# One version of an expert's last block, branch hints on TensorE, and row sums on TensorE in a decoder step

## The chip, the cores and the metric

The kernel runs on one core of a Trainium2 chip. The metric is the time of one execution on the device in microseconds (us). A core has TensorE (PE, with its weight loads PEld), VectorE (DVE), ScalarE (ACT), GpSimd (POOL), and SyncE (SP), which here only starts transfers. Each engine has its own stream of instructions, and they meet by semaphores.

## The reference

One step of a one-layer decoder for a prompt of 2048 rows and 8 x 4 sample rows, all of width 1024. The attention and the state-space part come first; the change touches what follows them, a mixture of experts and the final norm:

```python
grp = argmax(softmax(hf @ w_rc + b_rc));  top_v, top_i = top_k(fine logits of grp, 2)
eid = grp * 8 + top_i                     # two of 32 experts for each row
hid = silu(xb @ w_gate[e]) * (xb @ w_up[e]);  ys = hid @ w_down[e]      # widths 1024 -> 512 -> 1024
y = sum of a row's two expert rows, times their gates
x = x + gate * y                          # gate: a vector from the conditioning
out = rms_norm(x, g_final)
```

## The kernel before

The expert stage (function `moe`) goes through the 32 experts in an order that the counts decide at run time. An expert's rows are cut into blocks of 128; `blocks[p]` is the number of rows of the p-th expert, read into a register of every engine. A block is 48 products into PU (`up`, 24 for each half `hf` of the hidden width), 24 into PO (`down`), 8 turns of the next block's rows (`turned`) and 4 of the hidden values (`hidT`). Every f32 product is three products in a faster format, so each weight unit is split into a high and a low part: ACT casts (L1940), DVE subtracts (L1941); `convert` does both, and after every second unit SP loads the next expert's part into the same buffer (`load`). An expert has 12 units. EARLY (0 to 3) and LATE (10, 11, of the expert before) can be converted only when the expert before is nearly through.

An expert with more than 128 rows first runs one to three blocks by `further` (branches L2109, L2111, L2113), then its last block by `main(p, True)`. An expert with at most 128 rows runs `main(p, False)` in the Else branch, a second copy of the same 84 PE instructions. The two copies differ in this: with several blocks the first `further` block has already converted the six units LATE and EARLY. Tile's framework counts semaphores the same on every path: where an `If` is skipped, each engine raises the counts that the skipped instructions would have raised. Instructions stand in the order of the code on each engine (a manual schedule).

Stored rows go to Y_d by POOL's indirect transfers. The last stage (function `final`) takes 17 tiles of 128 rows (the last has 32): DVE adds the two rows of each row's experts (L2258) and multiplies by the gate (L2259), POOL adds x (L2260; DVE in the last three tiles), ACT sums the squares (L2265), DVE and POOL make 1/rms (L56, L58), DVE scales (L2270), and ACT's queue stores. It is a pipeline of three tiles: `add(n)`, `square(n - 1)`, `store(n - 2)`.

Of the kernel before, what the change touches and what calls it, by code (L numbers as in the profile page):

```python
# [12 lines left out]
F32 = mybir.dt.float32  # L13
# [4 lines left out]
ALU = mybir.AluOpType  # L18
AX = mybir.AxisListType
PSUM = bass.MemoryType.PSUM  # L20
# [1861 lines left out]
STEPS = (), (0, 1, 2, 3, 4, 5), (6,), (7,), (), (), (8, 9)  # L1882
EARLY = 0, 1, 2, 3
BOTH, AT0, AT1 = 4, 6, 1
LATE = 10, 11


class Experts:
# [20 lines left out]
    def load(self, p, i):  # L1909

        if p >= 32:
            self.after(i)
            return
        if not self.ready:
            self.later.append((p, i))
            return
        if i in (0, 5):
            self.now = self.K.nc.sync.value_load(self.R.order[0:1, p:p + 1], min_val=0, max_val=31)
        load_w(self.K, self.I, self.RAW[i], bass.ds(self.now, 1), i)

# [9 lines left out]
    def convert(self, p, u, hi, lo):  # L1930

        h = u % 2
        raw = self.RAW[u // 2]
        wh, wl = self.unit(p, u)
        if u < 8:
            raw = raw.rearrange("p (j k f) -> p j k f", j=2, k=2)[:, :, h]
            wh, wl = (t.rearrange("p (j f) -> p j f", j=2) for t in (wh, wl))
        else:
            raw = raw[:, 1024 * h:1024 * h + 1024]
        hi(wh, raw)  # L1940
        lo.tensor_tensor(out=wl, in0=raw, in1=wh.bitcast(F32), op=ALU.subtract)  # L1941
        if h:
            self.load(p + 1, u // 2)


def moe(K, I, E, first, h2_d, Y_d, R, TK, last):
# [4 lines left out]
    tc, nc = K.tc, K.nc  # L1951
    V, G, A = nc.vector, nc.gpsimd, nc.scalar
    NE = 32
    with ExitStack() as st:
# [15 lines left out]
        def convert(p, us):  # L1970
            for u in us:
                if p < NE:
                    E.convert(p, u, A.copy, V)
# [54 lines left out]
            nc.gpsimd.indirect_dma_start(out=Y_d, out_offset=bass.IndirectOffsetOnAxis(ap=R.dst[:, col:col + 1], axis=0),  # L2028
                                         in_=Y, in_offset=None, bounds_check=2 * TK - 1, oob_is_err=False)

        def block(p, before, x, steps):


            for k in range(BOTH):
                up(p, 0, (k,))
                up(p, 1, (k,))
            steps[0]()
            if before is not None:
                store(before)
            steps[1]()  # L2040
            up(p, 0, range(BOTH, 8))
            act(0)
            if x is not None:
                turned(x)
            steps[2]()
            up(p, 1, range(BOTH, AT0))
            hidT(0)
            up(p, 1, range(AT0, 8))
            steps[3]()
            act(1)  # L2050
            steps[4]()
            if x is not None:
                prepare()
            steps[5]()
            for c in range(AT1):
                down(p, c)
            hidT(1)
            steps[6]()
            for c in range(AT1, 4):
                down(p, c)  # L2060
# [4 lines left out]
        def further(p, b):  # L2065


            steps = [nothing] * 7
            if b == 0:
                steps[0] = lambda: convert(p, LATE)  # L2070
                steps[1] = lambda: convert(p + 1, EARLY)
            else:
                steps[1] = lambda: gather(R.src[:, 32 * (b + 1) + p:32 * (b + 1) + p + 1], X1)
            before = 32 * (b - 1) + p if b else 96 + p - 1
            block(p, before if p or b else None, X1, steps)

        def count(p):
            if p < NE:
                blocks[p] = nc.values_load(R.cnt[0:1, p:p + 1], min_val=0, max_val=2080)

        def main(p, several):

            def step(i):
                def run():
                    if i == 0 and not several:
                        convert(p, LATE)
                    elif i == 1:
                        gather_second(p + 1)
                    elif i == 2:
                        gather_first(p + 2)  # L2090
                    convert(p + 1, [u for u in STEPS[i] if not (several and u in EARLY)])
                return run

            block(p, 64 + p if p or several else None, X0 if p + 1 < NE else None, [step(i) for i in range(7)])

        gather(R.src0, X0)
        E.begin()
# [5 lines left out]
        blocks = {}  # L2103
        count(0)
        for p in range(NE):
            if p == NE - 1:
                last()
            count(p + 1)
            with tc.If(blocks[p] > 128) as several:  # L2109
                further(p, 0)  # L2110
                with tc.If(blocks[p] > 256):  # L2111
                    further(p, 1)
                    with tc.If(blocks[p] > 384):  # L2113
                        further(p, 2)
                main(p, True)
            with several.Else():
                main(p, False)
        store(96 + NE - 1)


# [116 lines left out]
def final(K, F, Y_d, TK, O):  # L2237
    tc, nc = K.tc, K.nc
    V, G, A = nc.vector, nc.gpsimd, nc.scalar
    with ExitStack() as st:  # L2240
        q = st.enter_context(tc.tile_pool(name="oq", bufs=10, reuse_waits="tile"))
        sm = st.enter_context(tc.tile_pool(name="os", bufs=4, reuse_waits="tile"))
        jk = q.tile([128, 1024], BF, name="jk", bufs=1)
        gfin, gate = F.place(0), [F.place(1), F.place(2)]
        tiles = {}

        def loads(n):
            t = F.seq[n]
            r = NS if t == 16 else 128
            y = [q.tile([128, 1024], F32, name=f"y{k}") for k in range(2)]  # L2250
            for k in range(2):
                nc.sync.dma_start(out=y[k][:r], in_=Y_d[TK * k + 128 * t:TK * k + 128 * t + r])  # L2252
            x = F.place(3 + n) if n < 9 else F.more[n - 9]
            tiles[n] = t, r, x, y

        def add(n):
            t, r, x, y = tiles[n]
            V.tensor_tensor(out=y[0][:r], in0=y[0][:r], in1=y[1][:r], op=ALU.add)  # L2258
            V.tensor_tensor(out=y[0][:r], in0=y[0][:r], in1=gate[t == 16][:r], op=ALU.mult)  # L2259
            (V if n > 13 else G).tensor_tensor(out=x[:r], in0=x[:r], in1=y[0][:r], op=ALU.add)  # L2260

        def square(n):
            t, r, x, y = tiles[n]
            ss = sm.tile([128, 1], F32, name="ss")
            A.activation(jk[:r], x[:r], AF.Square, accum_out=ss[:r])  # L2265
            rs[n] = rstd_of(K, sm, ss[:r], D)

        def store(n):
            t, r, x, y = tiles.pop(n)
            V.scalar_tensor_tensor(out=x[:r], in0=x[:r], scalar=rs.pop(n)[:r], in1=gfin[:r], op0=ALU.mult, op1=ALU.mult)  # L2270
            dst = O['ys'] if t == 16 else O['yp'].rearrange("(n t) d -> t n d", t=16)[t]
            nc.scalar.dma_start(out=dst, in_=x[:r])  # L2272

        N, rs = len(F.seq), {}
        for n in range(10):
            loads(n)
        for n in range(N + 2):
            for f, m in ((add, n), (square, n - 1), (store, n - 2)):
                if 0 <= m < N:
                    f(m)  # L2280
            if n + 10 < N:
                loads(n + 10)
# [114 lines left out]
```

## Time and profile before

| | |
|---|---|
| median of 3 runs | 2761.41 us (2761.29 to 2764.57) |
| profiled execution, its own time | 2763.94 us |
| its span | 2762.1 us |
| busy: PE, DVE, ACT, POOL | 2389.0, 1472.9, 1153.3, 568.4 us |
| expert stage, first product to last | 1622.83 to 2649.2 us |
| last stage | from there to 2762.1 us |

The span is the time from the first to the last instruction that the profiler saw; the execution's own time lies 1.8 us above it. Matmuls overlap: a product of 512 columns has a record of 0.39 us, and the next starts 0.23 us after it. [...] "issue" as a releaser says that nothing in the profile explains the wait.

### The profile page before, as it was taken

Reading aid. Unit: us, or ns where it says so; the run is one execution under the profiler, and the core shown is the slowest. Engines: PE = TensorE matmul, PEld = TensorE weight load, DVE = VectorE, ACT = ScalarE, POOL = GpSimd, SP = SyncE. Lnnn points to the kernel's source line nnn. Section 1 sums busy time; section 2 is a strip of 40 time slices with the busy share of each in tenths; the row PEclk is TensorE's granted clock in tenths of the full one; section 3 lists DMA queues with packets and bytes.
Section 4 is the critical chain, followed back from the end, with each engine's and each line's share of the span. In section 5 each row is a group of like instructions: output and inputs, shape, how many; then the busy total and the mean of one; then the engine's idle time right before and its main releaser. Section 6 shows DMA issues by size and latency. Waiting matters only on the chain. (4 is left out here: it accounts for less than half of the span.)

```text
span 2762.1 us, 35592 instructions
## 1 busy us (share of the span) xinstructions
PE 2389.0 (86%) x11999; PEld 1886.4 (68%) x11999; DVE 1472.9 (53%) x2980; ACT 1153.3 (42%) x1885; POOL 568.4 (21%) x725
## 2 busy tenths in 40 slices
PE   6999999897699999997999768999999998898930
PEld 3766677663367799995777647777777777777720
DVE  4544311264153566635687673544754676656558
ACT  3222211232133455555344353444654566556411
POOL 0022100001002335452444211101110111101036
PEclk9999999898899999998999879999999999999975
DMA  7322211575744621114333463645855786677664
GB/s 271 91 104 105 93 58 54 184 240 180 204 138 141 197 63 35 30 39 150 122 125 125 163 234 112 237 152 206 292 196 186 277 299 250 243 267 259 247 225 179
DMA packets 239150, 467.92 MB, mean 169 GB/s; under 512 B 87620, under 2 KB 117492, under 8 KB 236799
## 3 DMA queue, kind: packets, MB, share of 16 engines
q1 hardware_dynamic: 211496, 411.95, 43.4%
q0 software_dynamic: 16160, 38.50, 4.0%
q10 hardware_dynamic: 11200, 13.83, 1.5%
q8 instruction: 150, 2.46, 0.4%
q14 instruction: 144, 1.18, 0.1%
HBM read 395.60 MB, written 87.92 MB: 175 GB/s over the span
## 5 line engine op out<-in xcount | busy, mean ns | idle before, releaser
L1941 DVE TENSOR_TENSOR wl<-raw,wh 128x1024 fp32r<-128x1024 f32 x384 | 451.8, 1222 | 151.4 <-ACT wh L1940 145.9
L1940 ACT CAST wh<-raw 128x1024 fp32r<-128x1024 f32 x384 | 381.2, 1050 | 43.5 <-PE pu L2006 39.5
L2006 PE MATMUL pu<-wh,xh 128*128 128x512 f32 x816 | 340.8, 418 | 66.7 <-issue 52.6
L2006 PE MATMUL pu<-wl,xh 128*128 128x512 f32 x816 | 329.9, 404 | 5.0 <-issue 5.0
L2006 PE MATMUL pu<-wh,xl 128*128 128x512 f32 x816 | 329.3, 404 | 0.0
L2006 PEld LDWEIGHTS pu<-wh,xh 128*128 128x128 f32 x816 | 158.7, 195 | 110.9 <-issue 77.9
L206 PE MATMUL po<-wh,hh 128*128 128x512 f32 x512 | 208.6, 408 | 12.1 <-ACT hh L133 12.1
L206 PE MATMUL po<-wl,hh 128*128 128x512 f32 x512 | 206.9, 404 | 0.0
L206 PE MATMUL po<-wh,hl 128*128 128x512 f32 x512 | 202.7, 401 | 0.0
L2028 POOL DMA_INDIRECT Y_d<-y,Rdst x51 | 58.7, 1152 | 632.4 <-ACT y L2027 616.5
L2006 PEld LDWEIGHTS pu<-wl,xh 128*128 128x128 f32 x816 | 159.0, 195 | 37.1 <-issue 5.4
L2006 PEld LDWEIGHTS pu<-wh,xl 128*128 128x128 f32 x816 | 158.5, 194 | 37.1
L873 DVE CUSTOM_DVE_ANT_0 jk<-pa,mask 128x256 bf16<-128x256 f32 (+1 forms) x384 | 118.0, 362 | 113.7 <-PE pa L870 112.7
L2010 DVE TENSOR_TENSOR hid<-hid,pu 128x256 f32<-128x256 f32 x102 | 42.7, 419 | 241.8 <-ACT hid L2009 241.8
L2023 PE MATMUL po<-wh,hh 128*128 128x512 f32 x408 | 164.9, 404 | 0.0
L2023 PE MATMUL po<-wh,hl 128*128 128x512 f32 x408 | 160.3, 393 | 0.0
L2023 PE MATMUL po<-wl,hh 128*128 128x512 f32 x408 | 160.3, 393 | 0.0
L939 PE MATMUL pb<-QS,KH 128*128 128x256 f32 (+1 forms) x384 | 150.4, 398 | 0.0
L216 ACT COPY ob<-po 128x512 f32<-128x512 f32 x64 | 37.6, 587 | 264.1 <-PE po L206 262.2
L2009 ACT ACTIVATE hid<-pu 128x256 f32<-128x256 f32 x102 | 39.3, 385 | 254.1 <-PE pu L2006 253.4
L942 ACT ACTIVATE PT<-pb 128x512 f32<-128x512 f32 (+1 forms) x152 | 89.9, 591 | 120.3 <-PE pb L940 119.1
L940 PE MATMUL pb<-QM,KL 65*128 65x256 f32 (+1 forms) x384 | 139.2, 370 | 0.9 <-DMA QM<-MR 0.9
(586 smaller groups left out, 5035.1 us busy)
## 6 DMA issues: line engine op xcount, KB each, us to landing
raw<-w_expert_gate SPq DMA_DIRECT2D x128, 512.0 KB
raw<-w_expert_up SPq DMA_DIRECT2D x128, 512.0 KB
raw<-w_expert_down SPq DMA_DIRECT2D x64, 1024.0 KB
y<-Y_d SPq DMA_DIRECT2D x32, 512.0 KB
kr<-cache_k_win SPq DMA_DIRECT2D x56, 256.0 KB
kr<-cache_v_win SPq DMA_DIRECT2D x56, 256.0 KB
vb<-out_vp SPq DMA_DIRECT2D x96, 128.0 KB
wada<-w_ada_ffn SPq DMA_DIRECT2D x24, 512.0 KB
```

Of the source, the lines that this page charges most:

```text
L206: nc.tensor.matmul(out, a[:, kt, :], wt[c][:, kt], start=(kt == 0 and i == 0), stop=(kt == 7 and i == len(terms) - 1))
L873: V.tensor_tensor_reduce(out=jk[:, o:o + n], in0=pt[:, o:o + n], in1=mask[:, 256 - n:256], op0=ALU.add, op1=ALU.max, scale=1.0, scalar=-3e ...
L939: nc.tensor.matmul(po, cols(KH, c0, step, 128), cols(QS, c0, step, nq), start=True, stop=False)
L940: nc.tensor.matmul(po, cols(KL, c0, step, 128), cols(QM, c0, step, nq), start=False, stop=True)
L942: A.activation(PT[:, :o], ps[:, :o], AF.Exp)
L1940: hi(wh, raw)
L1941: lo.tensor_tensor(out=wl, in0=raw, in1=wh.bitcast(F32), op=ALU.subtract)
L2006: nc.tensor.matmul(PU[hf], x[:, k, :], y, start=(k == 0 and j == 0), stop=(k == 7 and j == 2))
L2009: A.activation(HID[hf], PU[hf][:, 0:256], AF.Silu)
L2010: V.tensor_tensor(out=HID[hf], in0=HID[hf], in1=PU[hf][:, 256:512], op=ALU.mult)
L2023: nc.tensor.matmul(PO[i], x[:, c % 2, :], y[:, cs], start=(c == 0 and j == 0), stop=(c == 3 and j == 2))
L2028: nc.gpsimd.indirect_dma_start(out=Y_d, out_offset=bass.IndirectOffsetOnAxis(ap=R.dst[:, col:col + 1], axis=0), in_=Y, in_offset=None, bou ...
```

## The change

The Else copy is gone. `main(p)` follows the `If` for every expert, and the six units LATE and EARLY are converted in it under a condition of their own (`alone`), in its first step; it always stores the block before. TensorE gets a hint instruction in each block behind which a branch on a count follows, with the count's comparison in a register. In the last stage PE adds the two expert rows by products with the unit matrix into PSUM (`both`), DVE multiplies from PSUM, and DVE adds x in all tiles; POOL has only the power left.

```diff
@@ -1914,7 +1914,7 @@
         if not self.ready:
             self.later.append((p, i))
             return
-        if i in (0, 5):
+        if i in (0, 2, 5):
             self.now = self.K.nc.sync.value_load(self.R.order[0:1, p:p + 1], min_val=0, max_val=31)
         load_w(self.K, self.I, self.RAW[i], bass.ds(self.now, 1), i)
 
@@ -2028,7 +2028,7 @@
             nc.gpsimd.indirect_dma_start(out=Y_d, out_offset=bass.IndirectOffsetOnAxis(ap=R.dst[:, col:col + 1], axis=0),
                                          in_=Y, in_offset=None, bounds_check=2 * TK - 1, oob_is_err=False)
 
-        def block(p, before, x, steps):
+        def block(p, before, x, steps, label, hint):
 
 
             for k in range(BOTH):
@@ -2052,6 +2052,8 @@
             if x is not None:
                 prepare()
             steps[5]()
+            if label:
+                tc.mark_branch_hint_location(label, hint=hint, engines=[mybir.EngineType.PE])
             for c in range(AT1):
                 down(p, c)
             hidT(1)
@@ -2072,26 +2074,33 @@
             else:
                 steps[1] = lambda: gather(R.src[:, 32 * (b + 1) + p:32 * (b + 1) + p + 1], X1)
             before = 32 * (b - 1) + p if b else 96 + p - 1
-            block(p, before if p or b else None, X1, steps)
+            at = 128 * (b + 2)
+            block(p, before if p or b else None, X1, steps, f"at{at}_{p}" if b < 2 else None, blocks[p] > at)
 
         def count(p):
             if p < NE:
                 blocks[p] = nc.values_load(R.cnt[0:1, p:p + 1], min_val=0, max_val=2080)
 
-        def main(p, several):
+        def main(p):
+
+            def alone():
+                with tc.If(blocks[p] <= 128):
+                    convert(p, LATE)
+                    convert(p + 1, EARLY)
 
             def step(i):
                 def run():
-                    if i == 0 and not several:
-                        convert(p, LATE)
+                    if i == 0:
+                        alone()
                     elif i == 1:
                         gather_second(p + 1)
                     elif i == 2:
                         gather_first(p + 2)
-                    convert(p + 1, [u for u in STEPS[i] if not (several and u in EARLY)])
+                    convert(p + 1, [u for u in STEPS[i] if u not in EARLY])
                 return run
 
-            block(p, 64 + p if p or several else None, X0 if p + 1 < NE else None, [step(i) for i in range(7)])
+            block(p, 64 + p, X0 if p + 1 < NE else None, [step(i) for i in range(7)],
+                  f"at128_{p + 1}" if p + 1 < NE else None, blocks[p + 1] > 128 if p + 1 < NE else None)
 
         gather(R.src0, X0)
         E.begin()
@@ -2106,15 +2115,13 @@
             if p == NE - 1:
                 last()
             count(p + 1)
-            with tc.If(blocks[p] > 128) as several:
+            with tc.If(blocks[p] > 128, label=f"at128_{p}"):
                 further(p, 0)
-                with tc.If(blocks[p] > 256):
+                with tc.If(blocks[p] > 256, label=f"at256_{p}"):
                     further(p, 1)
-                    with tc.If(blocks[p] > 384):
+                    with tc.If(blocks[p] > 384, label=f"at384_{p}"):
                         further(p, 2)
-                main(p, True)
-            with several.Else():
-                main(p, False)
+            main(p)
         store(96 + NE - 1)
 
 
@@ -2240,6 +2247,7 @@
     with ExitStack() as st:
         q = st.enter_context(tc.tile_pool(name="oq", bufs=10, reuse_waits="tile"))
         sm = st.enter_context(tc.tile_pool(name="os", bufs=4, reuse_waits="tile"))
+        ps = st.enter_context(tc.tile_pool(name="ops", bufs=4, space=PSUM, reuse_waits="tile"))
         jk = q.tile([128, 1024], BF, name="jk", bufs=1)
         gfin, gate = F.place(0), [F.place(1), F.place(2)]
         tiles = {}
@@ -2253,11 +2261,19 @@
             x = F.place(3 + n) if n < 9 else F.more[n - 9]
             tiles[n] = t, r, x, y
 
+        def both(n):
+
+            t, r, x, y = tiles[n]
+            zs[n] = ps.tile([128, 1024], F32, name="z")
+            for h in range(2):
+                cs = slice(512 * h, 512 * h + 512)
+                for k in range(2):
+                    nc.tensor.matmul(zs[n][:r, cs], K.ident[:r, :r], y[k][:r, cs], start=(k == 0), stop=(k == 1))
+
         def add(n):
             t, r, x, y = tiles[n]
-            V.tensor_tensor(out=y[0][:r], in0=y[0][:r], in1=y[1][:r], op=ALU.add)
-            V.tensor_tensor(out=y[0][:r], in0=y[0][:r], in1=gate[t == 16][:r], op=ALU.mult)
-            (V if n > 13 else G).tensor_tensor(out=x[:r], in0=x[:r], in1=y[0][:r], op=ALU.add)
+            V.tensor_tensor(out=y[0][:r], in0=zs.pop(n)[:r], in1=gate[t == 16][:r], op=ALU.mult)
+            V.tensor_tensor(out=x[:r], in0=x[:r], in1=y[0][:r], op=ALU.add)
 
         def square(n):
             t, r, x, y = tiles[n]
@@ -2271,11 +2287,12 @@
             dst = O['ys'] if t == 16 else O['yp'].rearrange("(n t) d -> t n d", t=16)[t]
             nc.scalar.dma_start(out=dst, in_=x[:r])
 
-        N, rs = len(F.seq), {}
+        N, rs, zs = len(F.seq), {}, {}
         for n in range(10):
             loads(n)
+        both(0)
         for n in range(N + 2):
-            for f, m in ((add, n), (square, n - 1), (store, n - 2)):
+            for f, m in ((both, n + 1), (add, n), (square, n - 1), (store, n - 2)):
                 if 0 <= m < N:
                     f(m)
             if n + 10 < N:
```

Three places in the order of instructions, without times. The first is PE where a single expert's block begins (the Else copy before; wh0 is the high part of a weight unit, xh the rows). Before:

```order
L2023 MATMUL po1_13300<-wh11_13283,hh1_13309 128x512
L2023 MATMUL po1_13300<-wl11_13284,hh1_13309 128x512
L2023 MATMUL po1_13300<-wh11_13283,hl1_13310 128x512
L2109 UNCONDITIONAL_BRANCH
L2006 MATMUL pu0_13297<-wh0_12952,xh_13301 128x512
L2006 MATMUL pu0_13297<-wl0_12953,xh_13301 128x512
```

and now, at the end of the skipped `If` and the start of `main`:

```order
L2023 MATMUL po1_13300<-wl11_13284,hh1_13309 128x512
L2023 MATMUL po1_13300<-wh11_13283,hl1_13310 128x512
L2122 UNCONDITIONAL_BRANCH
L2122 UNCONDITIONAL_BRANCH [waits PE_49]
L2120 UNCONDITIONAL_BRANCH [waits PE_49]
L2118 UNCONDITIONAL_BRANCH [waits PE_49]
L2006 MATMUL pu0_13297<-wh0_12952,xh_13301 128x512 [waits DVE_49,Activation_49]
L2006 MATMUL pu0_13297<-wl0_12953,xh_13301 128x512
```

The Else copy began with its first product and no wait; now the path that skips L2118 ends in a row that waits for PE's own semaphore, so for its products before, and `main` follows.

The second is PE in the middle of a single expert's block, where the products into PO begin. Before:

```order
L2006 MATMUL pu1_13298<-wh7_12947,xh_13301 128x512
L2006 MATMUL pu1_13298<-wl7_12948,xh_13301 128x512
L2006 MATMUL pu1_13298<-wh7_12947,xl_13302 128x512
L2023 MATMUL po0_13299<-wh8_13277,hh0_13307 128x512 [waits Activation_49]
L2023 MATMUL po0_13299<-wl8_13278,hh0_13307 128x512
```

and now:

```order
L2006 MATMUL pu1_13298<-wh7_12947,xh_13301 128x512
L2006 MATMUL pu1_13298<-wl7_12948,xh_13301 128x512
L2006 MATMUL pu1_13298<-wh7_12947,xl_13302 128x512
L2056 REGISTER_ALU
L2403 BRANCH_PREFETCH_HINT
L2023 MATMUL po0_13299<-wh8_13277,hh0_13307 128x512 [waits Activation_49]
L2023 MATMUL po0_13299<-wl8_13278,hh0_13307 128x512
```

A comparison of the next count and the hint stand ahead of the last 24 products of the block.

The third is ACT at a single expert's first casts (raw5 holds LATE, raw0 and raw1 hold EARLY; DMAHW are the semaphores of SP's transfers). Before:

```order
L1940 CAST wh0_12952<-raw4_12791 128x1024 [waits DMAHW6_49]
L1940 CAST wh1_12954<-raw4_12791 128x1024
L2109 UNCONDITIONAL_BRANCH
L1940 CAST wh6_12945<-raw5_12793 128x1024 [waits DMAHW5_49]
L1940 CAST wh7_12947<-raw5_12793 128x1024
L2027 ACTIVATE y_13305<-po0_13299,Rg_76 128x512 [waits DMASW3_49,DMASW2_49,DMASW5_49,PE_49,Activation_49]
L2027 ACTIVATE y_13305<-po1_13300,Rg_76 128x512 [waits PE_49,Activation_49]
L1940 CAST wh8_13277<-raw0_12779 128x1024 [waits DMAHW7_49,DMAHW6_49]
```

and now:

```order
L2118 UNCONDITIONAL_BRANCH [waits Activation_49]
L2087 COMPARE_AND_BRANCH
L1940 CAST wh6_12945<-raw5_12793 128x1024 [waits DMAHW1_49,DVE_49,DMAHW6_49,PE_49,Activation_49]
L1940 CAST wh7_12947<-raw5_12793 128x1024 [waits DVE_49,PE_49,Activation_49]
L1940 CAST wh8_13277<-raw0_12779 128x1024 [waits DMAHW2_49,DMAHW3_49,DMAHW0_49,DMAHW7_49,DVE_49,Activation_49]
L1940 CAST wh9_13279<-raw0_12779 128x1024 [waits DVE_49,Activation_49]
L1940 CAST wh10_13281<-raw1_12782 128x1024 [waits DMAHW2_49,DMAHW4_49,DMAHW1_49,DMAHW5_49,DVE_49,Activation_49]
L1940 CAST wh11_13283<-raw1_12782 128x1024 [waits DVE_49,Activation_49]
```

The casts of LATE waited for one transfer. They now wait also for DMAHW6, DVE and PE, whose counts SP, DVE and PE raise for the skipped `If`; the two ACTIVATEs that empty PO stand behind the six casts and no longer between them. SP's row for the skipped `If` (L2118) waits for SP_sequencer and five of its transfer semaphores.

## Rows read from the trace of the kernel before

**Rows 1.** Two stages: length, busy of PE PEld DVE ACT POOL, PEclk, DMA, GB/s.

```profile
1616.00:2649.60 1033.60, 953.25 (x4280) 763.08 (x4278) 586.51 (x696) 549.16 (x784) 115.17 (x100) 0.97 0.65 233
2649.60:2762.00 112.40, 0.00 (x0) 0.00 (x0) 94.68 (x71) 20.29 (x36) 70.91 (x32) 0.51 0.62 228
```

**Rows 2.** Waits of PE, 1600 to 2660: who, releaser, us in total, times, longest us.

```profile
PE pu L2006 <- issue: 57.7, 20, 5.0
...
PE pu L2006 <- PEq L2111: 5.9, 7, 1.9
...
PE pu L2006 <- PEq L2113: 1.1, 2, 0.5
```

**Rows 3.** Branch lines L2109 and L2111: count, ns min/median/max, first and last start.

```profile
L2109 PEldq COMPARE_BRANCH  x44: 70/310/6798, 1615.9 to 2646.5; - x44
...
L2109 POOLq INC_SWDGE_SEM  x20: 581/1022/1457, 1635.0 to 2566.4; - x20
...
L2111 PEldq COMPARE_BRANCH  x12: 65/1833/4585, 1658.8 to 2627.4; - x12
```

**Rows 4.** Timeline of PE at block starts: start, us, operation, [idle before, releaser].

```profile
1719.97 0.51 PE L2006 MATMUL pu<-wh,xh 128*128 128x512 f32 x1 [3.41 <-issue]
...
1725.51 0.80 PE L2006 MATMUL pu<-wl,xh 128*128 128x512 f32 x1 [5.03 <-issue]
...
1865.09 0.50 PE L2006 MATMUL pu<-wh,xh 128*128 128x512 f32 x1 [1.70 <-issue]
...
2553.94 0.80 PE L2006 MATMUL pu<-wh,xh 128*128 128x512 f32 x1 [3.76 <-issue]
...
2593.85 0.47 PE L2006 MATMUL pu<-wh,xh 128*128 128x512 f32 x1 [0.30 <-PEq L2111]
```

**Rows 5.** Short stretches behind a branch, within a block, and of one block.

```profile
1843.00:1846.70 3.70, 3.68 (x9) 2.91 (x10) 3.27 (x3) 2.45 (x3) 0.00 (x0) 0.55 1.02 395
1847.00:1850.40 3.40, 3.40 (x16) 2.81 (x15) 2.23 (x2) 1.05 (x1) 0.00 (x0) 1.00 0.98 375
...
1865.10:1883.50 18.40, 18.15 (x84) 14.75 (x85) 14.76 (x18) 13.07 (x18) 4.06 (x3) 1.00 1.00 375
```

**Rows 6.** Timeline of ACT, SP, DVE and PE around the block from 1865.09.

```profile
1861.45 1.99 ACT L1940 CAST wh<-raw 128x1024 fp32r<-128x1024 f32 x2
...
1863.02 2.68 SPq L1877 DMA_DIRECT2D raw<-w_expert_down  x2
...
1865.57 6.90 DVE L1941 TENSOR_TENSOR wl<-raw,wh 128x1024 fp32r<-128x1024 f32 x6 [0.31 <-ACT wh L1940]
...
1875.64 0.38 PE L2014 MATMUL pt<-ident,hid 128*128 128x128 f32 x2
```

**Rows 7.** Line L2109 on SP, from 1862 to 1868.

```profile
L2109 SPq COMPARE_BRANCH  x1: 55/55/55, 1864.0 to 1864.0; - x1
```

**Rows 8.** Timeline of the last stage: its first add, one of 13 slow tiles, the end.

```profile
2658.16 1.22 DVE L2258 TENSOR_TENSOR y<-y,y 128x1024 f32<-128x1024 f32 x1 [11.21 <-DMA y<-Y_d]
...
2682.03 3.38 POOL L2260 TENSOR_TENSOR raw<-raw,y 128x1024 f32<-128x1024 f32 x1 [0.93 <-DVE ms L56]
2683.13 3.36 DVE L2258 TENSOR_TENSOR y<-y,y 128x1024 f32<-128x1024 f32 x1
...
2742.32 1.22 DVE L2258 TENSOR_TENSOR y<-y,y 128x1024 f32<-128x1024 f32 x1
...
2747.23 1.21 DVE L2258 TENSOR_TENSOR y<-y,y 32x1024 f32<-32x1024 f32 x1
...
2749.72 1.21 DVE L2260 TENSOR_TENSOR x<-x,y 32x1024 f32<-32x1024 f32 x1
```

**Rows 9.** Timeline of PE: two f32 products of an earlier stage.

```profile
697.83 0.38 PE L700 MATMUL pt<-sa,UT 128*128 128x128 f32 x2
698.05 0.60 PE L701 MATMUL pt<-sb,HP 128*128 128x256 f32 x2
```

**Rows 10.** Group of instructions: DVE operation that reads PSUM; busy us, mean ns, idle before.

```profile
L134 DVE TENSOR_TENSOR xl<-pt,xh 128x512 fp32r<-128x512 f32 x102 | 65.5, 683 | 1.1
```

## The prediction

> **What bounds the kernel now.** I read the busy times of the two stages first, then PE's waits in the expert stage, then the branches behind them, then the blocks one by one, and last the final stage.
>
> The expert stage lasts 1033.6 us with PE busy for 953, while DVE and ACT are busy for little over half of it [rows 1]: PE bounds it, and what PE waits for is the loss. PE's waits there are mostly "issue": 57.7 us in 20 waits, then 5.9 and 1.1 us that its own sequencer ends at L2111 and L2113 [rows 2]. They are the branches on the counts. A branch that falls through takes PE's sequencer 70 ns, one that jumps to the far Else copy 4 to 6 us [rows 3]. The sequencer runs some 2 us ahead of the array, so part is hidden. Of 32 experts 12 reach L2111 and so have several blocks; POOL evens its counts 20 times, once for each single expert [rows 3]. A single expert behind an expert with several blocks finds PE idle for 3.4 to 3.8 us (ten such starts; the first and the last are shown), one behind another single expert for about 1.7 [rows 4]. One wait of 5.03 us is not at a branch but one product behind a jump [rows 4].
>
> A long wait costs twice. Behind it the granted clock is 0.55 and PE starts 9 products in 3.7 us, where it starts 16 in 3.4 at 1.0 [rows 5]: 9 would take 1.9, so 1.8 us are lost. After the short waits this doesn't happen (1.00 in the block from 1865.1) [rows 5].
>
> The last stage, 112 us, is bound by DVE, busy for 94.7; PE does nothing there and its clock is at the lower level [rows 1]. While POOL adds x (3.38 us), DVE's first addition beside it takes 3.36, where it takes 1.22 when POOL doesn't add [rows 8].
>
> **The branches on PE: what goes.** Idle time: 57.7 + 5.9 + 1.1 - 5.0 (the wait that isn't at a branch) = 59.7 us. Lower clock: 10 x 1.8 = 18. Together 77.7 us, if every branch found its target in time. The hint stands ahead of 24 products of 0.23 us, so 5.6 us, and some turns, before the block's end; the jumps took 4.1 to 5.9 us, at most 6.8 [rows 3]. That is just enough. The trace of before has no hint, so its effect is bounded by nothing and by all of it. The middle copy's branch (L2087) is a short one inside a block and hidden by the sequencer's lead; without that cover it would cost 0.3 us each, 10 us in all.
>
> **What comes in its place.** First, the path that skips the `If` now waits for PE's own products. The nearest rows are the skips at L2111 and L2113: 0.30 us idle where the branch was quick [rows 4], 0.55 and 0.84 on the mean of [rows 2]. I take 0.5: 20 single experts and 10 skips at 256 and 384 rows give 15 us.
>
> Second, and this the diff doesn't show: the casts of LATE in a single expert wait for a count that SP raises when it skips. SP comes there late, since it stands in order behind the load of raw4. Around the block from 1865.09 PE ended the block before at about 1863.4 (1865.09 less 1.70) [rows 4]; call this T. SP issued raw4 at 1863.02 and passed the branch at 1864.0 [rows 6, 7], T + 0.6. Jump and counting I put at 0.5 (no row shows it; POOL's counting takes 1.0 [rows 3], nothing is the other end). So the casts begin at T + 1.1; before they began at 1861.45 [rows 6], T - 1.95. DVE's eight subtractions (LATE, EARLY, units 4 and 5) stand ahead of its first product of the hidden values. At 1.15 us each [rows 6], one cast of 1.0 behind the first, they end at T + 11.3, and with 0.4 for that product hidT can start at T + 11.7. PE would reach hidT 10.55 us after the block's start [rows 6], so at T + 11.0. It waits 0.7, with POOL's price for the counting 1.2; I take 1.0 for 20 blocks: 20 us. The bounds are nothing and 1.6 us each. Behind DVE in that block nobody else waits: EARLY is used a block later, and PO, which ACT now empties after the six casts, is needed only 12 us into the block.
>
> The expert stage: 77.7 - 15 - 20 = 43 us less. The duties of the several-block path (the same casts, the same loads) are as before.
>
> If the hints did nothing, every single expert would pay the short wait of 1.7 (the jump over the Else copy, which makes ten of them long, is gone in any case): 10 x 2.0 + 18 = 38 us go, 4 come, and SP's lateness hides in the wait. That is 34 us less: the two outcomes lie close.
>
> **The last stage.** PE adds the rows by four products of 512 columns with f32 operands. An earlier f32 product of 128 columns took 0.22 us from start to start, in two records, at the full clock [rows 9]; four of 512 columns take 16 times that, 3.5 us for a tile, and 7.0 at the lower clock. DVE keeps three operations: the multiplication, now from PSUM, the addition of x, the scaling. A DVE operation from PSUM takes 0.68 us for 512 columns [rows 10], so 1.2 to 1.3 for 1024, as from SBUF. Without POOL's addition the last tiles take 4.91 us with four operations (2742.32 to 2747.23) [rows 8]; with three, 4.91 - 1.23 = 3.7. PE at 3.5 keeps ahead of that.
>
> Before: from the first addition at 2658.16 to the last at 2749.72 + 1.21, 92.8 us [rows 8]. After: the first product 7.0 us at the lower clock, 16 tiles at 3.7 to 3.85 (the operations end to end), and 2.5 for the last: 69 to 71. 23 us less, I take; the end behind it (11 us) stays. The transfers carry 26 MB in these 80 us; they ran at up to 395 GB/s [rows 5], so 66 us, which could take back some 5.
>
> **The sum.** 43 + 23 = 66. The profiled execution's own time, 2763.9, gives 2698; the median of the runs lies 2.5 below it: 2696 us.
>
> **The rivals.**
> - Hints without effect: 34 + 23, 2704 us. For it: the jump target is found by nothing that this trace shows. Against it: the sequencer passes the hint early enough. [...]
> - SP's lateness hidden: 20 us more gain, 2676. For it: DVE is busy 14.8 us of 18.4 in such a block [rows 5], so the order could bend less than I reckon.
> - PE's clock stays low in the last stage: 17 x 7.0 = 119 us from 2658.2, where DVE would have been through after 70; 49 us dearer, 2745. Against it: PE would then be busy without a pause, and after a pause of 4 us it was back at 1.0 within 4 us [rows 5].
> - Slower: SP, when it skips, waits for five of its transfer semaphores, among them the last loads of raw2. If these land later than SP comes, the casts, the subtractions and with them PE wait in each of 20 single experts. Between two single experts the DMA engines are full (share 1.00, 375 GB/s) [rows 5]. It decides from 66/20 = 3.3 us for each; at 5 us, 100 us come, and the kernel takes 2796. Against it: raw2 is loaded half a block before, about 9 us.
> [...]
>
> **How the numbers follow.** Forecast 0.45 (2685 to 2708 by its own bounds); hints without effect 0.17; SP's lateness hidden 0.16; clock low 0.07; the two slower ones 0.05 and 0.04; between them 0.06. 2668 to 2735 holds the first three with the bounds of the drain (15 us could be 6 to 25), of SP's wait and of the transfers. A measurement can tell 0.2%, 5.5 us, from no change. Faster by more: 0.89; within it 0.03; slower 0.08.
>
> **What would show it.** PE's waits on "issue" in the expert stage fall from 57.7 to under 15 us, and its branch at the new L2118 takes under 0.5 us in the median; if it stays at 4 us, the hints do nothing. In single experts hidT waits for DVE by about 1 us, and the cast of LATE starts after SP's skip, not 2 us before the block ends. The granted clock of the stage is 0.99 or more. In the last stage no DVE operation of 1024 columns takes over 1.4 us, a tile takes 3.7 to 3.9, and PE's clock is back at 1.0 by the third tile. I am wrong if PE's idle time moves into the blocks' middles (hints) or if SP's skip ends more than 2 us behind its branch.

## The result and the profile after

The changed kernel takes 2699.49 us (median of 4 runs, 2690.43 to 2700.78) where the kernel before took 2762.99 beside it: ratio 0.9754, 95% interval 0.972 to 0.9789, so 58 to 77 us less. The forecast was 2696 us, within 2668 to 2735.

The profiled execution's own time fell from 2763.9 to 2700.0 us. By stages: the expert stage took 1026.3 us from the start of its first product to the start of its last and takes 983.2, the last stage took 112.9 from there to the end and takes 87.7, and the expert stage begins 4.5 us later (1627.4 for 1622.8). That last part is hardly the change's: PE's program ahead of this point is the old one, and in the kernels below, which share it, the start lies anywhere from 1621.1 to 1628.2 (e3, where PE's first product waits longer by its own edit, aside). The sum is 43.1 + 25.2 - 4.5 = 63.8.

The expert stage of the kernel before, from its first product on, and the two stages of the changed kernel (columns as in [rows 1]):

```profile
1622.80:2649.40 1026.60, 952.38 (x4276) 762.77 (x4276) 579.98 (x681) 542.83 (x776) 112.91 (x98) 0.97 0.65 232
...
1627.00:2610.80 983.80, 938.69 (x4276) 749.20 (x4276) 574.48 (x681) 548.68 (x784) 132.56 (x100) 0.99 0.66 242
2610.80:2698.00 87.20, 61.52 (x137) 25.95 (x136) 62.05 (x68) 20.46 (x36) 25.02 (x18) 0.85 0.76 294
```

In the expert stage PE does the same products in 938.7 busy us, and PEclk, TensorE's granted clock as a share of full speed, is 0.99 (0.97 before). In the last stage DVE is busy for 62 us, and PE works. The waits in the expert stage, against [rows 2]: first ACT's for SP's count, then PE's; the row of `pt` and `hid` is hidT, the turns of the hidden values.

```profile
ACT wh L1940 <- SPq L2118: 58.8, 18, 4.1
...
PE pt L2014 <- DVE hid L2010: 28.6, 48, 4.2
PE pu L2006 <- PEq L2118: 15.0, 20, 6.0
...
PE pu L2006 <- PEq L2120: 3.9, 7, 0.6
PE pu L2006 <- PEq L2122: 1.9, 3, 0.7
PE pu L2006 <- issue: 1.3, 1, 1.3
```

and hidT before the change:

```profile
PE pt L2014 <- DVE hid L2010: 8.6, 31, 0.5
```

The waits on "issue" have gone from 57.7 to 1.3, and that one lies within a block, not at a branch. In their place stand PE's own sequencer (PEq) at the ends of the skipped `If`s and, longest of all, hidT behind DVE. The first of the 20 waits at L2118, 6.0 us, lies ahead of the stage's first product; before, that product waited 6.1 us for ACT. The branch itself, and its hint (columns as in [rows 3]):

```profile
L2118 PEldq COMPARE_BRANCH  x32: 77/368/6484, 1620.6 to 2572.1; - x32
...
L2118 PEldq EVENT_SEMAPHORE  x20: 51/51/51, 1627.1 to 2517.7; - x20
```

```profile
L2403 PEldq BRANCH_PREFETCH_HINT  x48: 28/35/42, 1644.1 to 2584.6; - x48
```

The median of all 32 passes is 0.37 us; 20 of them are jumps, with a median of 0.6 by themselves, and three of those take over 2 us (3.3, 5.1 and the first, 6.5, which no hint precedes). A hint takes 35 ns. Starts of blocks and of hidT, against [rows 4]:

```profile
1627.36 0.77 PE L2006 MATMUL pu<-wh,xh 128*128 128x512 f32 x1 [5.96 <-PEq L2118]
...
1643.97 0.44 PE L2014 MATMUL pt<-ident,hid 128*128 128x128 f32 x2 [4.18 <-DVE hid L2010]
...
1957.99 0.47 PE L2006 MATMUL pu<-wh,xh 128*128 128x512 f32 x1 [2.86 <-PEq L2118]
...
2284.97 0.48 PE L2006 MATMUL pu<-wh,xh 128*128 128x512 f32 x1 [0.30 <-PEq L2118]
...
2296.80 0.44 PE L2014 MATMUL pt<-ident,hid 128*128 128x128 f32 x2 [0.90 <-DVE hid L2010]
```

The usual start of a single expert waits 0.30 us (2284.97); from product to product it comes 0.69 us behind the last one where 0.23 is usual, so it costs 0.46. One start (1957.99) waits 2.86. The block from 2284.97 shows SP's part: when each engine comes to the skipped `If`, and what follows on SP, ACT and DVE.

```profile
L2118 SPq EVENT_SEMAPHORE  x6: 17/17/17, 2285.8 to 2286.2; - x6
...
L2118 DVEq EVENT_SEMAPHORE  x1: 21/21/21, 2284.4 to 2284.4; - x1
L2118 PEldq EVENT_SEMAPHORE  x1: 51/51/51, 2284.7 to 2284.7; - x1
L2118 SPq COMPARE_BRANCH  x1: 45/45/45, 2285.4 to 2285.4; - x1
```

```profile
2286.14 5.80 ACT L1940 CAST wh<-raw 128x1024 fp32r<-128x1024 f32 x6 [3.23 <-SPq L2118]
...
2287.22 9.20 DVE L1941 TENSOR_TENSOR wl<-raw,wh 128x1024 fp32r<-128x1024 f32 x8 [2.87 <-ACT wh L1940]
...
2284.38 5.62 SPq L1877 DMA_DIRECT2D raw<-w_expert_down  x2
```

PE ended the block before at 2284.67 (2284.97 less 0.30). DVE and PE counted by 2284.7; SP, behind the load of raw4 (2284.38), came at 2285.4 and counted until 2286.2, and only then ACT cast and DVE subtracted, to 2296.42; hidT waited 0.90. In the first block SP counted for longer: it came at 1627.4, and its last count was at 1630.3.

```profile
L2118 SPq EVENT_SEMAPHORE  x6: 17/17/17, 1628.0 to 1630.3; - x6
```

The last stage: DVE's three operations of one tile and the next tile's first, and then three stretches in the columns of [rows 1] (compare [rows 8]).

```profile
2639.13 1.22 DVE L2275 TENSOR_TENSOR y<-z,raw 128x1024 f32<-128x1024 f32 x1
2640.38 1.23 DVE L2276 TENSOR_TENSOR raw<-raw,y 128x1024 f32<-128x1024 f32 x1
...
2641.59 1.27 DVE L2286 SCALAR_TENSOR_TENSOR raw<-raw,rstd,raw 128x1024 f32<-128x1024 f32 x1
2642.78 1.22 DVE L2275 TENSOR_TENSOR y<-z,raw 128x1024 f32<-128x1024 f32 x1
```

```profile
2618.00:2626.00 8.00, 7.42 (x11) 3.15 (x12) 1.04 (x1) 0.00 (x0) 0.00 (x0) 0.63 1.01 409
2626.00:2634.00 8.00, 8.00 (x20) 3.61 (x19) 6.06 (x7) 2.30 (x4) 0.58 (x1) 1.00 1.03 410
2634.00:2642.00 8.00, 8.00 (x20) 3.50 (x19) 7.93 (x11) 2.30 (x4) 3.28 (x3) 1.00 1.02 411
```

A tile takes 3.65 us, no DVE operation of 1024 columns over 1.28, and the clock is at 1.0 from the second tile on.

### The profile page after: what moved, and what is told of

It reads as the page before. It is cut to its first block, busy times and chain, and to the rows that moved or that the text cites. A ratio compares the mean times of both kernels' runs of the same rounds, so it can differ in the third digit from the quotient of the medians.

```text
span 2698.3 us, 36856 instructions
## 1 busy us (share of the span) xinstructions
PE 2441.5 (90%) x12135; PEld 1903.2 (71%) x12135; DVE 1435.3 (53%) x2977; ACT 1155.7 (43%) x1889; POOL 541.9 (20%) x712
## 5 line engine op out<-in xcount | busy, mean ns | idle before, releaser
L1940 ACT CAST wh<-raw 128x1024 fp32r<-128x1024 f32 x384 | 381.1, 1049 | 75.5 <-SPq L2118 58.8
L2006 PE MATMUL pu<-wh,xh 128*128 128x512 f32 x816 | 333.3, 408 | 20.8 <-PEq L2118 15.0
L2006 PE MATMUL pu<-wh,xl 128*128 128x512 f32 x816 | 323.1, 396 | 1.3 <-issue 1.3
L2006 PE MATMUL pu<-wl,xh 128*128 128x512 f32 x816 | 322.5, 395 | 0.0
L2028 POOL DMA_INDIRECT Y_d<-y,Rdst x52 | 66.8, 1285 | 764.9 <-ACT y L2027 731.6
L988 PE MATMUL pw<-PT,vb 128*128 128x128 f32 (+1 forms) x752 | 132.1, 312 | 0.0
```

Source lines behind the costliest of these rows:

```text
L988: nc.tensor.matmul(out, vt[h, b, idx], PT[:, o + q0:o + q0 + n_], start=start, stop=(final and Wd == W), skip_group_check=True)
L2006: nc.tensor.matmul(PU[hf], x[:, k, :], y, start=(k == 0 and j == 0), stop=(k == 7 and j == 2))
```

## The experiments

Two quantities are compared throughout: the ratio to the kernel before (on the same chip in the same series) and, from the trace, the length of the expert stage from its first product to its last. The second comes from one trace of each kernel, so differences of a few us in it are not sure.

| kernel | expert stage, us | median, us | ratio to before, 95% |
|---|---|---|---|
| before | 1026.3 | 2762.99 | 1 |
| changed | 983.2 | 2699.49 | 0.9754 (0.972 to 0.9789) |
| e1 no hints | 1030.7 | 2746.79 | 0.9914 (0.9889 to 0.9938) |
| e2 hints only | 960.9 | 2706.77 | 0.9768 (0.9742 to 0.9794) |
| e3 casts ahead of the If | 1112.8 | 2832.75 | 1.0221 (1.0193 to 1.0248) |
| e4 hint late | 1023.8 | 2742.43 | 0.9898 (0.9872 to 0.9924) |
| e5 two copies, hints, new last stage | 965.2 | 2681.24 | 0.9686 (0.967 to 0.9702) |
| e6 SP's load behind the If | 969.7 | 2680.93 | 0.968 (0.9665 to 0.9694) |
| e7 hint early | 983.6 | 2696.97 | 0.9735 (0.9721 to 0.9748) |
| e8 POOL adds x | 985.5 | 2707.18 | 0.9775 (0.9761 to 0.9788) |
| e9 as e6, first expert too | 968.8 | 2684.12 | 0.968 (0.9657 to 0.9703) |
| e10 as e5, hint early | 961.0 | 2678.14 | 0.9653 (0.9631 to 0.9676) |

The kernel before ran at medians of 2768 to 2774 in the series of e1 to e10, so their ratios are to be read, not their times against 2699.

**e1_no_hints.** The changed kernel without its hints.

```diff
-            if label:
-                tc.mark_branch_hint_location(label, hint=hint, engines=[mybir.EngineType.PE])
```

> The new kernel without the hints; everything else as in it. Theory A (the prediction's: the hint lets PE's fetch of the jump target run beside the last products): without it the jump at L2118 is the short one everywhere, 1.7 us of idle PE at each of 20 single experts in place of 0.46, so +25 us of PE waits on its own sequencer; the wait of hidT on DVE (1.3 us in each of these blocks) then hides behind it, -20 to -25 us; sum 0 to +9, 2699 to 2708 us. Theory B (the hints do nothing, one version of the last block is the whole gain): 2699, and the idle time at L2118 stays at 0.46 each. Theory C (a jump without a hint costs what the far Else jump cost, 3.4 to 3.8 us, and the half clock behind it): +60 to +90, 2760 to 2790.

Measured: the expert stage is 4 us longer than before the change, and 47 longer than with hints. PE's waits and its branch:

```profile
PE pu L2006 <- PEq L2116: 60.4, 20, 6.1
PE pt L2014 <- DVE hid L2010: 11.0, 31, 2.9
```

```profile
L2116 PEldq COMPARE_BRANCH  x32: 76/4422/6591, 1617.9 to 2617.1; - x32
```

Apart from the first, the 19 waits are (60.4 - 6.1)/19 = 2.9 us each. Theory B falls. Theory A was right that hidT's wait hides behind the jump (11.0 us, near the 8.6 of before) and wrong about the jump: it isn't the short one but takes 4.4 us in the median of all 32 passes, 5.2 in that of the 20 jumps. The mean wait is near that of before, (57.7 - 5.0)/19 = 2.8, but it is spread the other way. By the timelines of the block starts the ten single experts behind one with several blocks waited 3.6 us before and wait 2.4 here, the nine behind another single expert 1.8 before and 3.4 here. The result lies between A and C.

**e2_hints_only.** The kernel before with hints and labels; the Else copy and the old last stage stay.

```diff
+            if label:
+                tc.mark_branch_hint_location(label, hint=hint, engines=[mybir.EngineType.PE])
             for c in range(AT1):
                 down(p, c)
...
-            with tc.If(blocks[p] > 128) as several:
+            with tc.If(blocks[p] > 128, label=f"at128_{p}") as several:
```

> The kernel before with the hints alone: two copies of the last block and the old last stage stay, the If has the label, the hint stands where the new kernel has it. Theory A (hints hide the fetch): the ten waits of 3.4 to 3.8 us and the ten of 1.7 at the start of single experts go, with the half clock behind the long ones; PE waits on its sequencer fall from 64 to under 15 us, the hidden values do not wait for DVE, since the casts stand where they stood: 60 to 75 us less, 2687 to 2703. Theory B (the far jump to the Else copy is what made the long waits and a hint does not help): 2762, waits as before.

Measured: 65.4 us less in the expert stage, as theory A has it, and 22.3 less than in the changed kernel. From the second block on PE's waits are:

```profile
PE pu L2006 <- issue: 16.1, 10, 2.4
PE pt L2014 <- DVE hid L2010: 8.1, 30, 0.3
PE pu L2006 <- PEq L2115: 2.1, 7, 0.3
PE pu L2006 <- PEq L2117: 1.7, 3, 0.6
```

hidT waits as before the change (8.3 us in the whole stage). With e1 the two parts of the change in the expert stage stand apart:

| expert stage, us | no hints | hints |
|---|---|---|
| two copies | 1026.3 | 960.9 |
| one version | 1030.7 | 983.2 |

The hints are worth 47 to 65 us; one version of the last block saves nothing with or without them and costs 22 with them (the 4 without them are too few to be sure).

**e3_alone_first.** The six casts ahead of the `If`.

```diff
+            alone(p)
             with tc.If(blocks[p] > 128, label=f"at128_{p}"):
```

> The new kernel with one step moved: the six casts of a single expert under their own condition stand ahead of the If on 128 rows, not in the first step of the block behind it, so that they no longer wait for SP's counting of the skipped If. Theory A (SP's lateness costs 1.3 us in each of 20 single experts and 4 us in the first block): hidT's wait on DVE falls from 28.6 us to under 4, 20 to 28 us less than the new kernel, 2672 to 2680. Theory B (DVE's six to eight subtractions are late whatever releases the casts): no change, 2695 to 2702. Theory C (the further branch on each engine, and PE's between hint and jump, costs as much as it frees): waits move to L2117, 2690 to 2710.

Measured: 130 us more in the expert stage, far beyond all three theories. hidT's wait is gone (8.5 us in 32), as A said, and another has come, by C's mechanism but far above its price: PE's first product waits for DVE's count.

```profile
PE pu L2006 <- DVEq L2117: 139.0, 20, 12.5
PE pt L2014 <- DVE hid L2010: 8.5, 32, 0.3
```

```profile
1958.39 9.17 DVE L1941 TENSOR_TENSOR wl<-raw,wh 128x1024 fp32r<-128x1024 f32 x8 [0.41 <-ACT wh L1940]
```

```profile
1967.77 0.77 PE L2006 MATMUL pu<-wh,xh 128*128 128x512 f32 x1 [6.71 <-DVEq L2117]
```

Eight subtractions (1958.39 to 1967.56), six of them moved ones, now stand on DVE ahead of the skipped `If`; DVE counts behind them, and PE starts 0.2 us later. It is SP's lateness once more, with another engine. What e3 was to show, e6 shows.

**e4_hint_late.** The hint ahead of the last 6 products instead of the last 24.

```diff
-            for c in range(AT1, 4):
-                down(p, c)
+            for c in range(AT1, 3):
+                down(p, c)
+            if label:
+                tc.mark_branch_hint_location(label, hint=hint, engines=[mybir.EngineType.PE])
+            down(p, 3)
```

> The new kernel with the hint moved from ahead of the last 24 products of a block to ahead of the last 6: 1.4 us ahead of the block's end and some 2 us of the sequencer's lead in place of 5.6 and some turns. Theory A (the hint starts a fetch of about 4 to 6 us that runs beside the products): only part of it is hidden now, 1 to 2 us of idle PE at L2118 in place of 0.46, of which hidT's wait on DVE takes back as much: the time 2700 to 2715, the waits on the sequencer +10 to +30 us. Theory B (the hint works by naming the target, not by its lead): waits as in the new kernel, 2699.

Measured: PE's waits at this branch rise from 15.0 to 58.3 us, and the stage is 7 us from that without hints.

```profile
PE pu L2006 <- PEq L2119: 58.3, 20, 6.1
PE pt L2014 <- DVE hid L2010: 12.7, 31, 4.6
```

```profile
L2119 PEldq COMPARE_BRANCH  x32: 77/3905/6600, 1620.4 to 2612.9; - x32
```

The 20 jumps take 4.7 us in the median, 5.2 without hints. So the lead is what counts (B falls). The fetch that A names stands in no trace, and A, which had part of the jump still hidden, put the loss too low: 1.4 us ahead is worth next to nothing (the medians of the runs, 2742 and 2747, lie 4 us apart).

**e5_hints_final.** e2 with the new last stage.

```diff
+        ps = st.enter_context(tc.tile_pool(name="ops", bufs=4, space=PSUM, reuse_waits="tile"))
...
+            for f, m in ((both, n + 1), (add, n), (square, n - 1), (store, n - 2)):
```

> The kernel before with the hints and the new last stage (row sums on PE), the two copies of the last block kept. Theory A (the parts add up: hints alone took 65.5 us from the expert stage, the new last stage 25): about 90 us less than the kernel before, 2670 to 2682, and 20 to 25 less than the new kernel, since single experts wait neither for PE's own products nor for SP. Theory B (the last stage's gain needs the new expert stage, or the transfers of the two collide): 2690 to 2706.

Measured: 2681.24 us, ratio 0.9686, in A's range. From the expert stage's last product to the end of the span it takes 88.5 us, as the changed kernel does (87.7), where e2 takes 112.8: the last stage's 24 us stand by themselves.

**e6_sp_early.** raw4's load moved to where SP has passed the `If`.

```diff
-        if h:
+        if h and not (self.hold and u // 2 == 4 and p + 1 < 32):
             self.load(p + 1, u // 2)
...
+        def held(p):
+            if 0 < p < NE - 1:
+                E.load(p + 1, 4)
...
-                steps[0] = lambda: convert(p, LATE)
+                steps[0] = lambda: (held(p), convert(p, LATE))
...
                 with tc.If(blocks[p] <= 128):
+                    held(p)
                     convert(p, LATE)
```

> The new kernel with SP's load of raw4 moved from ahead of the If on 128 rows to the first step behind it, in both paths (inside the If and under the condition of the six casts), so that SP comes to the If without waiting for DVE's last subtraction of the block before. Theory A (SP's count holds the casts; then PE's and DVE's counts hold them, at the end of PE's last product plus 0.5 us): the casts of LATE begin 0.6 to 0.9 us sooner, hidT's wait on DVE falls from 28.6 to 10 to 16 us, 10 to 20 us less than the new kernel, 2680 to 2690. Theory B (PE's or DVE's count comes as late as SP's): no change, 2696 to 2702. Theory C (raw4's load now comes later and its casts wait for it): PE waits in the second half of blocks, slower than 2702.

Measured: 13.5 us less in the expert stage, hidT's wait 15.4 us, both as A has it. What holds the casts now:

```profile
ACT wh L1940 <- PEq L2124: 27.1, 12, 4.5
PE pt L2014 <- DVE hid L2010: 15.4, 34, 3.8
ACT wh L1940 <- SPq L2124: 13.6, 4, 3.7
```

```profile
2272.50 5.79 ACT L1940 CAST wh<-raw 128x1024 fp32r<-128x1024 f32 x6 [1.93 <-PEq L2124]
```

In the changed kernel SP held ACT for 58.8 us. The block that answers to the one from 2284.97 begins here at 2272.62: SP comes to the `If` at 2269.0, PE's count releases the casts at 2272.50, 0.2 us behind the end of PE's last product (2272.32), and hidT waits for nothing there. In four blocks it is still SP that releases them, though it now comes early: in the block from 2214.88 it came at 2212.2, and its seven counts ended at 2216.3, 1.7 us behind PE's last product; hidT waited 1.39.

```profile
L2124 SPq EVENT_SEMAPHORE  x7: 17/17/17, 2212.6 to 2216.3; - x7
```

**e7_hint_early.** The hint 24 products behind a block's start.

> The new kernel with the hint moved the other way: from ahead of the last 24 products of a block to 24 products from its start, some 12 us ahead of the end in place of 5.6. Theory A (only the lead counts; 1.4 us was worth nothing, 5.6 nearly all): the rest goes, 2 to 8 us less, the branch at L2118 takes 0.4 us everywhere and no block ends with over 1 us of idle PE (the new kernel had 3.0 and 1.2 once each). [...]

Measured: the stage as in the changed kernel (983.6), the branch's median 0.36 us, PE's waits at this branch 15.0 us as there; nothing is won.

```profile
L2118 PEldq COMPARE_BRANCH  x32: 77/364/6903, 1617.6 to 2570.0; - x32
```

One start stays late, the one at 1957.99 in the changed kernel: by 3.3 us here, 3.0 there and 3.1 in e6, from product to product. The other late one (1.2 us) is gone. Why that one jump is late is open.

**e8_pool_adds.** The addition of x back on POOL for 14 tiles.

```diff
-            V.tensor_tensor(out=x[:r], in0=x[:r], in1=y[0][:r], op=ALU.add)
+            (V if n > 13 else G).tensor_tensor(out=x[:r], in0=x[:r], in1=y[0][:r], op=ALU.add)
```

> The new kernel with the addition of x back on POOL for the first 14 tiles, the row sums still on PE. Theory A (a DVE operation beside POOL's addition is held to its length, whatever it reads): one of the multiplication and the scaling takes 3.3 us in each of 14 tiles, a tile 4.6 to 4.9 us in place of 3.65, 14 to 18 us more than the new kernel. Theory B (the multiplication, which reads PSUM, is not held): all DVE operations take 1.2 to 1.3, and POOL's 3.4 and 1.45 us set the pace, 4.8 a tile, the same 16 us more. Theory C (POOL is quicker without a DVE addition beside it): PE's 3.45 a tile bounds, 2 to 4 us less.

Measured: 10.1 us more from the expert stage's last product to the end (97.8), less than the 14 to 18 of theory A; a tile takes 4.64. POOL and DVE in one tile:

```profile
2639.76 2.35 POOL L2276 TENSOR_TENSOR raw<-raw,y 128x1024 f32<-128x1024 f32 x1 [0.81 <-DVE y L2275]
```

```profile
2640.30 2.88 DVE L2286 SCALAR_TENSOR_TENSOR raw<-raw,rstd,raw 128x1024 f32<-128x1024 f32 x1
2643.11 1.21 DVE L2275 TENSOR_TENSOR y<-z,raw 128x1024 f32<-128x1024 f32 x1
```

The scaling takes 2.88 us where it takes 1.27 in the changed kernel, and it ends 1.1 us behind POOL's addition, not far from that 1.27; the four tiles that follow look the same (2.89 to 2.92, and 1.1 behind). So the scaling is as late as if the two took turns; how the one holds the other no run shows. POOL's addition takes 2.35 us here, where it took 3.38 beside two DVE operations [rows 8], so it, too, had probably been held there; that would be why A's 3.3 us for the held operation was too much, and no run tests it. Whether the multiplication, which reads PSUM, would be held as well stays open, since it never lay beside POOL's addition.

**e9_sp_first.** e6 for the first expert too.

> The kernel of e6 with raw4's load moved behind the If for the first expert too. Theory A (in the first block, too, SP's late count holds the casts: it took 26.9 us there, against 20.0 with two copies): SP comes to the first If some 3 us sooner, the block takes 22 to 25 us, 2 to 5 us less than e6, 2676 to 2679. Theory B (SP's counting of the first skip waits for the semaphores of its own transfers, which land when they land): no change, 2680, block 0 at 26 to 27.

Measured: no change (ratio 0.968 as e6), and the first block takes 26.0 us. Theory B holds, and the trace shows why:

```profile
L2124 SPq COMPARE_BRANCH  x1: 50/50/50, 1621.8 to 1621.8; - x1
L2124 SPq EVENT_SEMAPHORE  x7: 17/17/17, 1622.3 to 1628.7; - x7
```

SP comes to the `If` 3.6 us ahead of the block's first product (1625.44) and not 0.3 behind it as in e6, but its counts wait for the semaphores of its own transfers and end 3.3 us behind that product, much as in e6 (3.4). This is the wait of the prediction's rival on SP's transfer semaphores. It is met in the first expert, in the changed kernel too, and in four blocks of e6, but in no kernel does it come near 3.3 us in each of the 20 single experts, from where it would have decided.

**e10_two_copies_early.** e5 with the hint where e7 has it.

> The kernel of e5 (two copies, hints, new last stage) with the hint some 12 us ahead of a block's end in place of 5.6. With two copies, ten single experts behind one with several blocks still wait 1 to 2.6 us for their jump, 17 us in all, though the same hint stands ahead; single behind single waits for nothing. Theory A (those ten lack lead): the 17 us go, 2664 to 2670. [...]

Measured: PE's waits on "issue" behind the first block are 17.1 us in 11; nine of them are starts of single experts, the same nine as in e2 and e5.

```profile
PE pu L2006 <- issue: 17.1, 11, 2.2
```

Theory A falls: the 17 us stay, so lead isn't what these jumps lack. Eight of the nine come right behind a jump over the Else copy (two such starts, out of ten, don't wait), the ninth behind another single expert; so the unhinted jump just ahead goes with most of these waits and not with all. Why they wait stays open. At 2678.14 us, ratio 0.9653, this is the quickest of the kernels, though its interval overlaps those of e5, e6 and e9.

## Why the prediction was right

**The branches.** The step held in both halves. The 59.7 us of waits at branches went. PE's busy time, in which the lower clock shows, fell by 13.7 (952.4 to 938.7) where 18 were forecast. The one wait within a block, 5.0 us, which the forecast left standing, went but for one of 1.3; without hints it is 1.6 (e1), so the hints are not what shortened it. "Just enough" was right for the lead: 5.6 us hides the jump but for two starts, 1.4 us hides almost nothing (e4), 12 us no more than 5.6 (e7).

**PE's own products.** 15 us were forecast for 30 skips; there are 9.0 at L2118 without the first, 3.9 and 1.9, together 14.8. The sum is closer than its parts: the usual start of a single expert waits 0.30 us and not 0.5, and the two late jumps (2.86 and 1.02) fill it up.

**SP's lateness.** 20 us were forecast; hidT's wait grew from 8.6 to 28.6, by 20.0. That the two agree is in part luck: 4.2 are the first block's, which the sum had not singled out, and the rest is about 1.0 each in the 16 other blocks that wait, where 19 were reckoned. In the block shown, with T the end of PE's last product, SP came at T + 0.7 and the casts began at T + 1.5, where T + 0.6 and T + 1.1 had been reckoned. e6 shows the cause: with SP early 13.2 us of the 20 are gone, and PE's count is next in line. One sign that the prediction had named against itself did come, in the first block: SP's last count there is almost 3 us behind its branch (1627.4 to 1630.3), beyond the 2 us of the sign; in the block shown it is 0.8.

**The last stage.** 23 us were forecast, 25.2 came: 3.65 us a tile (3.7 to 3.85), the first products at PEclk 0.50 (2619 to 2623), and 1.00 from the second tile on. The 7.0 us put down for a first tile wholly at the lower clock no run shows: from its first product to DVE's multiplication it took 6.4 (2618.58 to 2624.95). DVE waited twice for PE in the first tiles (0.95 and 0.89 us) and twice for a square of ACT's that came late (1.04 and 0.84). That a DVE operation is longer beside POOL's addition shows in e8, too: 2.9 us for 1.27.

The 43 us of the forecast and the 43.1 measured agree better than the terms: PE's busy time gave 4 us less than was put down for the lower clock, the wait that was left out gave 4 us more.

**What was wrong** is a rival's price. "Hints without effect" was put at 2704 us, since every single expert would then pay "the short wait of 1.7". Without hints the kernel gains 0.9%, not 2%, and that in the last stage: a jump costs 2.9 us of idle PE in the mean, as with two copies (2.8), and PEclk is back at 0.97 with it (e1; 0.99 with hints). That the far Else copy made the long jumps, and that taking it away would save 34 us by itself, was the error: the ten starts behind several blocks did become shorter, by 1.2 us each, but the nine others became longer by 1.6. The forecast didn't rest on it, since the hints worked. It hid, though, that the two parts of the change work against each other: the hints alone take 65 us, and one version gives 22 of them back, 20 of them in hidT's wait behind SP's count (28.6 us against 8.3 in e2). With SP's load moved (e6) the stage is 4.5 us from that of two copies with the same last stage (969.7 against 965.2), and the runs take the same time (2680.93 and 2681.24).

## What to carry to other kernels

Where a sequencer's jumps show as idle time of a busy engine, as PE's did here, a hint some 6 us ahead is a cheap cure to try first (35 ns each here, for 47 to 65 us less in the stage), and doubling or merging code is a separate decision to be measured by itself. A skipped conditional of this framework is a meeting point: each engine raises its counts there in its own order, so whatever stands ahead of it on any engine (a load that waits on SP, behind which ACT waited 58.8 us; subtractions on DVE, behind which PE waited 139.0 in e3) delays all who wait for that count; put such work behind the conditional, in both paths, as e6 did. In the last stage VectorE's scaling took 2.9 us beside GpSimd's addition and 1.27 without it, and sharing the additions between the two cost 10 us (e8); moving the sum of the rows to TensorE, which had stood idle, saved 15 even so (112.9 to 97.8).

## What was unexpected in the hardware

One might expect a hint that comes 1.4 us ahead of the block's end, in place of 5.6, to be worth a quarter as much. It is worth nearly nothing: the branch's median is 3.9 us against 4.4 without hints and 0.37 with the full lead (each over all 32 passes). A hint placed some 12 us ahead still serves (0.36). With two copies a hinted jump right behind an unhinted one can still take 4.3 us where the same hint serves elsewhere (0.36):

```profile
L2113 PEldq COMPARE_BRANCH  x3: 353/358/4267, 1714.8 to 1737.5; - x3
```

These are, in e2, the jump over the Else copy (1714.8, 0.35 us), the hinted one behind it (4.27) and a hinted one between two single experts (1737.5, 0.36).
